# Down projection of 32 of 43 FFN tiles in seven-product blocks, with weight forms as sums

## The chip, the cores and the metric

The kernel runs on one core of one Trainium2 chip. The metric is the device time of one execution in microseconds, the median of several runs.

## What is computed

One step of a one-layer decoder trunk for 544 tokens (512 of a prompt and 8 x 4 of a decode batch), all in f32: a token-mixing sub-layer with one input and one output projection, cross-attention into memory tokens, and a gated feed-forward layer (FFN) with a causal convolution, each between two norms. The change concerns the last product of the FFN:

```python
def conv_ffn(x, prev, w_up, w_conv, w_down):
    h = x @ w_up
    ext = jnp.concatenate([prev.astype(h.dtype), h], axis=1)
    hc = causal_dwconv(ext, w_conv)
    g, u = jnp.split(hc, 2, axis=-1)
    return (jax.nn.silu(g) * u) @ w_down, ext[:, -(FFN_CONV_WIDTH - 1):]
```

D_MODEL is 2048 and D_FF is 5504, so w_down has 43 tiles of 128 rows and 16 tiles of 128 columns.

## The kernel before

Activations lie transposed, 128 features x 544 tokens in a tile. Every f32 operand of a matmul is split into a high and a low part in TensorE's own 32-bit format (L80 `split`: ScalarE (ACT) copies the high part, L82, VectorE (DVE) subtracts it for the low part, L83). A product takes three matmuls: high weight with high token, high with low, low with high (L156 `mm6`, its matmul is L162). The 544 tokens go through in two halves, so a weight tile costs six matmuls.

Weights stream from memory through SyncE's (SP's) DMA queue into four raw buffers of 256 KB, and are split ahead of their use (L91 `Weights`, L116 its load); `pair_tiles` (L88) gives four pairs of 128 x 1024 tiles for the parts.

The up projection of tiles 6 to 42 already works in units of seven products in place of eight (Strassen's scheme): L1102 loads 512 KB weight quarters, L1110 forms their sums on DVE, L1154 is its matmul with 272 tokens at a time, L1134 to L1168 take the products out of PSUM. The results, the gated tiles f of the FFN, go to a buffer in DRAM (fd) and come back when wanted (fr).

The down projection then runs over blocks of FFN tiles (8, 8, 8, 8, 7 and 4; `BLOCKS`). For each of 16 output chunks m, a PSUM tile `dn` of two banks collects a block: 8 tiles x 3 x 2 matmuls. In the first block ACT copies it into the SBUF accumulator `facc[m]` (L1244), in the next four DVE adds it there (L1246). `hidden` (L1209) loads and splits the next block's f tiles. The last block, of 4 tiles (`dl`), is followed by the final norm, the residual and the output. The order within each engine's queue is set when the program is built, by a scheduler; an engine takes its queue strictly in order, and PSUM tiles are ordered as whole tiles: work on one bank of a tile waits for an earlier read of its other bank. `background` and `spend` (L144) hand out work beside matmuls by a budget of estimated microseconds.

Of the kernel before, what the change touches and what calls it, by code (L numbers as in the profile page):

```python
# [22 lines left out]
KD = DM // P  # L23
# [4 lines left out]
NF = DFF // P  # L28
LAST = ((0, 288), (288, NT))
FB = 8  # L30
BLOCKS = (8, 8, 8, 8, 7, 4)
NMEM = 256
EPS = 1e-6
RAW, WHL = 4, 8
NH = NT // 2
# [9 lines left out]
def trunk_kernel(ctx: ExitStack, tc: tile.TileContext, I, O):  # L45
    nc = tc.nc
    dma = nc.sync.dma_start
# [3 lines left out]
    wp = ctx.enter_context(tc.tile_pool(name="wp", bufs=1))  # L51
# [28 lines left out]
    def split(hi, lo, src, scale=None):  # L80
        if scale is None:
            nc.scalar.activation(hi, src, AF.Copy)  # L82
            nc.vector.tensor_tensor(lo, src, hi.bitcast(F32), op=ALU.subtract)  # L83
        else:
            nc.scalar.activation(hi, src, AF.Copy, scale=scale)
            nc.vector.scalar_tensor_tensor(lo, src, scale, hi.bitcast(F32), op0=ALU.mult, op1=ALU.subtract)  # L86

    def pair_tiles(name):  # L88
        return tuple(wp.tile([P, 1024], F32R, tag=f"w{x}", bufs=WHL // 2, name=f"{name}{x}") for x in "hl")

    class Weights:  # L91
# [6 lines left out]
        def add(self, src, kind="split", n=512, fresh=False):  # L98
            self.specs.append((src, kind, n, fresh))
# [32 lines left out]
    W = Weights()  # L132
# [3 lines left out]
    background = []  # L136

    def pause(cost):

        return cost, lambda: None  # L140
# [146 lines left out]
    add_project(wup, warm_up[:-3], 3)  # L287
    add_project(wup, warm_up[-3:], 3)

    def add_down():  # L290
        for bi, blk in enumerate(blocks):
            if blk is blocks[-1]:
                for m in range(KD):
                    W.add(I["w_down"][9, m], "split" if m < WHL else "mov", fresh=m == 0)
            else:
                for ms in [range(3)] + [[m] for m in range(3, KD)]:
                    for kc in range(2):
                        for m in ms:
                            if len(blk) == FB or kc == 0:
                                W.add(I["w_down"][bi * 2 + kc, m])  # L300
                            else:
                                W.add(I["w_down_3"][m], n=3 * P)


    xs = [None] * KD
# [404 lines left out]
    q = [None] * NG  # L710
# [201 lines left out]
    facc = [None] * KD  # L912
    fd = [dram.tile([P, NT], F32, name=f"fd{i}") for i in range(NF)]
# [80 lines left out]
    todo = [(kc * 4 + kk, 1) for kc in range(4) for kk in range(4)]  # L994
    for si, (hf, kc) in enumerate(seq):
# [5 lines left out]
        for at, (kk, g) in enumerate(steps):  # L1001
            k = kc * 4 + kk
# [36 lines left out]
    def halves(t):  # L1039
        return t.rearrange("p (a t) -> p a t", a=2)  # L1040
# [146 lines left out]
    load(WARM)  # L1187
    todo = list(order)
    for at, (i, n) in enumerate(order):
        while len(order) - len(todo) < min(at + 4, len(order)):  # L1190
            make(*todo.pop(0))
        product(i, n)
        if i == NF - 1:
            if n == "S1":
                for j in range(8):
                    f_load(j)
            for j in {"S2": (0, 1), "A12": (2, 3), "S3": (4, 5), "A22": (6, 7)}.get(n, ()):
                f_split(j)
            if n == "A22":
                add_down()  # L1200
                W.fill(W.used + 5)
    fastp.close()


    down = ctx.enter_context(ExitStack())
    resp[0] = down.enter_context(tc.tile_pool(name="resp2", bufs=1, reuse_waits="tile"))
    aux16[0] = down.enter_context(tc.tile_pool(name="facc", bufs=1, reuse_waits="tile"))

    def hidden(bi):  # L1209
        fss[bi] = []  # L1210
        for i in blocks[bi]:
            f = tmp(f"fr{i}")[:, :NT]
            dma(f, fd[i])
            fss[bi].append(tuple((res if bi == len(blocks) - 1 else mov)(f"f{x}{i}", F32R) for x in "hl"))
            split(*fss[bi][-1], f)

    for bi, blk in enumerate(blocks):
        nb = len(blk)
        if bi + 1 < len(blocks):
            hidden(bi + 1)  # L1220
        fs = fss[bi]

        if bi < len(blocks) - 1:
            grp = list(range(3))
            pss = [mm_ps(f"dn{bi}_{m}") for m in grp]
            for kc in range(2):
                ws = [W.next() for m in grp]
                for kk in range(min(4, nb - kc * 4)):
                    k = kc * 4 + kk
                    for w, ps in zip(ws, pss):  # L1230
                        mm6(ps, w, fs[k], k == 0, k == nb - 1, kk)
            for m in range(KD):
                if m < 3:
                    ps = pss[m]
                else:
# [6 lines left out]
                if bi == 0:  # L1242
                    facc[m] = auxu(f"facc{m}")
                    nc.scalar.activation(facc[m], flat(ps), AF.Copy)  # L1244
                else:
                    nc.vector.tensor_tensor(facc[m], flat(ps), facc[m], op=ALU.add)  # L1246
        else:


# [1 line left out]
            wl = [W.next() for m in range(4)]  # L1251
# [46 lines left out]
            for half in LAST:  # L1298
                a, b = half
# [16 lines left out]
                for ms in pairs:  # L1316
                    ps = mm_ps(f"dl{ms[0]}_{a}")
# [125 lines left out]
```

## Time and profile before

| what | value |
|---|---|
| median of 3 runs | 2319.52 us (2318.92 to 2319.97) |
| the profiled execution's own time | 2319.19 us |
| its span in the trace | 2317.5 us |
| PE busy | 2270.2 us (98%) |
| DVE busy | 1535.1 us (66%) |
| ACT busy | 931.5 us (40%) |
| POOL busy | 418.0 us (18%) |
| mean DMA rate | 119 GB/s |

The profile is one execution; its time lies .33 us under the median. The span is what the trace covers, 1.7 us less than that execution's time. PE is TensorE's matmuls, PEld its weight loads, POOL is GpSimd, SP is SyncE. Shares are averages over all stages; a stage's own bound is read from a stretch of it.

### The profile page before, as it was taken

Reading aid. Unit: us, or ns where it says so; the run is one execution under the profiler, and the core shown is the slowest. Engines: PE = TensorE matmul, PEld = TensorE weight load, DVE = VectorE, ACT = ScalarE, POOL = GpSimd, SP = SyncE. Lnnn points to the kernel's source line nnn. Section 1 sums busy time; section 2 is a strip of 40 time slices with the busy share of each in tenths; the row PEclk is TensorE's granted clock in tenths of the full one; section 3 lists DMA queues with packets and bytes.
Section 4 is the critical chain, followed back from the end, with each engine's and each line's share of the span. In section 5 each row is a group of like instructions: output and inputs, shape, how many; then the busy total and the mean of one; then the engine's idle time right before and its main releaser. Section 6 shows DMA issues by size and latency. Waiting matters only on the chain.

```text
span 2317.5 us, 43666 instructions
## 1 busy us (share of the span) xinstructions
PE 2270.2 (98%) x17755; PEld 2245.8 (97%) x17755; DVE 1535.1 (66%) x2401; ACT 931.5 (40%) x1526; POOL 418.0 (18%) x516
## 2 busy tenths in 40 slices
PE   8999999999999999999999999999999999999995
PEld 8999999999989889999999999999999999999995
DVE  6775494543495888788888888888887233342347
ACT  6221222443354554445545555554545232131133
POOL 0000000000041453133233323333331000000005
PEclk9999999999999999999999999999999999999997
DMA  7323323333454555333333333333335333232242
GB/s 230 95 83 80 89 84 88 86 113 97 141 174 146 160 178 188 101 121 105 120 120 109 108 120 124 99 121 115 115 105 193 97 121 127 94 112 88 85 160 78
DMA packets 149065, 276.31 MB, mean 119 GB/s; under 512 B 30880, under 2 KB 42432, under 8 KB 148864
## 3 DMA queue, kind: packets, MB, share of 16 engines
q1 hardware_dynamic: 148864, 273.53, 38.0%
q8 instruction: 139, 2.28, 0.4%
q14 instruction: 62, 0.51, 0.1%
HBM read 249.81 MB, written 23.66 MB: 118 GB/s over the span
## 4 chain that ended last, share of the span: by engine, by line
PE 90%; DVE 5%; DMA 2%; issue 1%; ACT 1%; POOL 0%; SPq 0%; POOLq 0%; DVEq 0%; ACTq 0%
PE mm L162 31%; PE ab L1154 24%; PE dn L162 20%; PE c L1154 9%; PE dl L162 1%; PE xo L162 1%; PE kps L162 1%; PE sps L792 1%; DVE fxl L86 1%; DVE mix L823 1%; DVE mix L669 0%; DMA fr<-fd 0%; DVE xa L822 0%; PE sop L881 0%; DMA raw<-in_w_xq 0%
## 5 line engine op out<-in xcount | busy, mean ns | idle before, releaser
L1246 DVE TENSOR_TENSOR facc<-dn,facc 128x544 f32<-128x544 f32 x64 | 46.0, 723 | 213.8 <-PE dn L162 213.7
L941 POOL COPY fe<-fst 128x16 f32<-128x16 f32 x86 | 181.3, 2120 | 0.0
L951 POOL COPY fnp<-fe 128x2 f32<-128x2 f32 x86 | 42.4, 493 | 613.1 <-DVE fe L1138 531.6
L956 DVE SCALAR_TENSOR_TENSOR fa<-fe,fcw,fa 128x560 f32<-128x560 f32 x172 | 136.6, 795 | 0.5 <-ACT fa L954 0.3
L234 POOL TENSOR_TENSOR r_f<-r_f,mhalf 128x3 f32<-128x3 f32 (+1 forms) x2 | 1.6, 777 | 500.2 <-DVE r_f L233 500.2
L386 DVE SCALAR_TENSOR_TENSOR y<-eb,cv,y 128x512 f32<-128x512 f32 x120 | 88.6, 738 | 0.0
L954 ACT ACTIVATE fa<-fe,fcw 128x560 f32<-128x560 f32 x86 | 65.7, 764 | 38.2 <-DVE fe L1139 28.9
L261 POOL TENSOR_TENSOR ss<-ss,sq_h 128x544 f32<-128x544 f32 (+2 forms) x45 | 55.8, 1241 | 70.7 <-ACT sq_h L260 70.0
L950 POOL COPY fns<-fe 128x16 f32<-128x16 f32 x86 | 58.0, 674 | 6.6 <-DVE fe L985 0.8
L958 ACT ACTIVATE fa<-fa 128x560 f32<-128x560 f32 x43 | 28.9, 673 | 47.6 <-DVE fa L956 47.5
L1110 DVE TENSOR_TENSOR S<-A,A 128x1024 f32<-128x1024 f32 x37 | 45.4, 1226 | 1.2
L1110 DVE TENSOR_TENSOR A<-A,S 128x1024 f32<-128x1024 f32 x37 | 45.3, 1224 | 1.2
L1110 DVE TENSOR_TENSOR A<-A,A 128x1024 f32<-128x1024 f32 x37 | 45.1, 1218 | 0.0
L1110 DVE TENSOR_TENSOR S<-S,A 128x1024 f32<-128x1024 f32 x37 | 45.0, 1216 | 0.0
L234 POOL TENSOR_TENSOR r_gn<-r_gn,mhalf 128x5 f32<-128x5 f32 x4 | 4.7, 1170 | 179.4 <-DVE r_gn L233 179.4
L1138 DVE TENSOR_TENSOR fe<-c,u 128x240 f32<-128x240 f32 x74 | 29.7, 402 | 3.6 <-ACT u L1134 3.5
L261 POOL TENSOR_TENSOR ss<-ss,sq_xa 128x256 f32<-128x256 f32 (+1 forms) x26 | 23.0, 886 | 48.0 <-ACT sq_xa L260 47.9
L83 DVE TENSOR_TENSOR fl<-fr,fh 128x544 fp32r<-128x544 f32 x43 | 29.0, 720 | 3.3 <-ACT fh L82 3.3
L82 ACT ACTIVATE fh<-fr 128x544 fp32r<-128x544 f32 x43 | 27.3, 653 | 7.6 <-DMA fr<-fd 4.8
L1134 ACT ACTIVATE u<-ab 128x272 f32<-128x272 f32 x74 | 28.1, 380 | 4.9 <-PE ab L1154 4.9
L963 DVE TENSOR_TENSOR f<-fa,fa 128x512 f32<-128x512 f32 x43 | 29.4, 684 | 0.0
L388 DVE SCALAR_TENSOR_TENSOR y<-eb,cv,y 128x32 f32<-128x32 f32 x120 | 28.6, 239 | 0.0
(3958 smaller groups left out, 9333.5 us busy)
## 6 DMA issues: line engine op xcount, KB each, us to landing
A<-in_w_up SPq DMA_DIRECT2D x148, 512.0 KB, 3.5
raw<-in_w_down SPq DMA_DIRECT2D x160, 256.0 KB, 2.7
raw<-in_w_in SPq DMA_DIRECT2D x128, 256.0 KB, 2.7
raw<-in_w_out SPq DMA_DIRECT2D x64, 256.0 KB, 2.7
raw<-in_w_up SPq DMA_DIRECT2D x48, 256.0 KB, 2.9
fd<-f SPq DMA_DIRECT2D x43, 272.0 KB, 2.1
fr<-fd SPq DMA_DIRECT2D x43, 272.0 KB, 4.6
raw<-in_w_xo SPq DMA_DIRECT2D x32, 256.0 KB, 2.9
```

Of the source, the lines that this page charges most:

```text
L162: nc.tensor.matmul(ps[:, pa:pb], lhsT=a_, rhs=b_[:, a:b], start=start and q == 0, stop=stop and q == 2)
L261: (eng or nc.vector).tensor_tensor(dst, dst, sq[:, :n], op=ALU.add)
L386: nc.vector.scalar_tensor_tensor(acc[:, :NP], e[:, t:t + NP], w, acc[:, :NP], op0=ALU.mult, op1=ALU.add)
L941: nc.gpsimd.tensor_copy(smp6(e)[:, :, 0:2], st[:, j, gu])
L950: nc.gpsimd.tensor_copy(nst[:, j, gu], smp6(e)[:, :, 4:6])
L951: nc.gpsimd.tensor_copy(nsp[:, j, gu], e[:, NP:NP + 2])
L954: nc.scalar.activation(acc, e[:, 0:560], AF.Copy, scale=fcw[:, m, 0:1])
L956: nc.vector.scalar_tensor_tensor(acc, e[:, t:560 + t], fcw[:, m, t:t + 1], acc, op0=ALU.mult, op1=ALU.add)
L1110: nc.vector.tensor_tensor(out, a, b, op=op)
L1138: nc.vector.tensor_tensor(e[:, 2 + NH:2 + NP], bank[:, :NP - NH], add[:, :NP - NH], op=ALU.add)
L1154: nc.tensor.matmul(bank, lhsT=w[:, k * P:(k + 1) * P], rhs=t, start=start and k == 0 and q == 0, stop=k == 7 and q == 2, skip_group_check= ...
L1246: nc.vector.tensor_tensor(facc[m], flat(ps), facc[m], op=ALU.add)
```

## The change

`BLOCKS` becomes (7, 8, 8, 8, 8, 4). The first block, of 7 tiles, runs as before with ACT's copy into `facc`, the last block runs as before too. The four blocks of 8 tiles between them run as 16 units (block, q), q = 0 to 3, each for four output chunks. A unit takes its weights as four quarters A11, A12, A21, A22 of 128 x 1024 (512 KB), and the token halves of the tiles as four others, and makes seven products of 24 matmuls x 272 tokens in the order A12, D, G, A11, E, H, A21, in place of eight. The weight forms are sums:

- S is loaded as A21, and a DMA issued by POOL adds A22 into it in flight; D is S. E is A12 with A22 added in the same way (L1256 of the new text).
- G is S + A12, added on DVE (L1261).
- H is that sum + A11, added by a third accumulating DMA (L1265), issued behind G's split.

The products of a unit gather in two two-bank PSUM tiles (`da`: A12, G, E, A21; `db`: A11) and, for D and H, in two one-bank tiles `dc`; half p of `da` and `db` is one bank. ACT takes every half out with a sign (L1291, L1300), DVE adds the results into `facc` (L1294, L1301). The next block's token forms, seven high and low pairs for each of two tile pairs, are made beside units q = 2 and 3 (`fd_form`). The down weights lie in DRAM in a new order (`w_down_s`); a unit reads A12, A21 and A22 twice, and A11 twice.

```diff
-BLOCKS = (8, 8, 8, 8, 7, 4)
+BLOCKS = (7, 8, 8, 8, 8, 4)
...
+    def fd_form(bi, d, n):
+        x, y = halves(fr[bi][d]), halves(fr[bi][2 + d])
+        b11, b12, b21, b22 = x[:, :, :NH], x[:, :, NH:], y[:, :, :NH], y[:, :, NH:]
+        if n == 1:
+            nc.vector.scalar_tensor_tensor(b22, b22, -1.0, b21, op0=ALU.mult, op1=ALU.subtract)
+        if n == 2:
+            nc.vector.tensor_tensor(b22, b11, b22, op=ALU.add)
+        if n == 4:
+            nc.vector.tensor_tensor(b21, b21, b11, op=ALU.subtract)
+        if n == 6:
+            nc.vector.scalar_tensor_tensor(b22, b22, -1.0, b12, op0=ALU.mult, op1=ALU.subtract)
+        src = (b22, b22, b22, b12, b21, b11, b22)[n]
+        TD[bi, n, d] = h, l = mov(f"d{n}h{d}", F32R), mov(f"d{n}l{d}", F32R)
+        nc.scalar.activation(halves(h), src, AF.Copy)
+        nc.vector.tensor_tensor(halves(l), src, halves(h).bitcast(F32), op=ALU.subtract)
...
+    dsteps = ("A12", "D", "G", "A11", "E", "H", "A21")
...
+    def d_load(u):
+        for n, *parts in (("A12", "A12"), ("S", "A21", "A22"), ("A11", "A11"), ("E", "A12", "A22"), ("A21", "A21")):
+            t = draws[u, n] = rawd.tile([P, 1024], F32, tag="rawd", bufs=8, name=f"{n}_{u[0]}_{u[1]}")
+            dma(t, d_src(u, parts[0]))
+            for a in parts[1:]:
+                nc.gpsimd.dma_start(t, d_src(u, a), accum_op=ALU.add)
+
+    def d_make(u, n):
+        s = draws[u, "S"]
+        if n == "G":
+            nc.vector.tensor_tensor(s, s, draws[u, "A12"], op=ALU.add)
+        dmade[u, n] = pair_tiles(f"{n}_{u[0]}_{u[1]}")
+        split(*dmade[u, n], s if n in ("D", "G", "H") else draws[u, n])
+        if n == "G":
+            nc.gpsimd.dma_start(s, d_src(u, "A11"), accum_op=ALU.add)
+
+    def d_product(u, n):
...
+        which = {"A11": "b", "D": "c", "H": "c"}.get(n, "a")
+        for p in range(2):
+            m = 4 * q + 2 * p
+            t = dbank[u, which]
+            bank = t[p][:, :NH] if which == "c" else t[:, p * 512:p * 512 + NH]
+            for k in range(4):
+                th, tl = (t_[:, k % 2 * NH:(k % 2 + 1) * NH] for t_ in TD[bi, dsteps.index(n), k // 2])
+                for i, (w, t) in enumerate(((wh, th), (wh, tl), (wl, th))):
+                    nc.tensor.matmul(bank, lhsT=w[:, (4 * p + k) * P:(4 * p + k + 1) * P], rhs=t,
...
+            for at, (u, n) in enumerate(dorder):
+                while len(dorder) - len(todo) < min(at + 4, len(dorder)):
+                    i = units.index(todo[0][0])
+                    while loaded <= min(i + (todo[0][1] == "E"), len(units) - 1):
+                        d_load(units[loaded])
+                        loaded += 1
+                    d_make(*todo.pop(0))
+                d_product(u, n)
+                if u[0] + 1 < len(blocks) - 1:
+                    if u[1] == 1 and n == "A12":
+                        fd_in(u[0] + 1)
+                    if u[1] == 2 and n == "G":
+                        for _, f in fd_work(u[0] + 1, [0]):
+                            f()
+                    if u[1] == 3 and n != "A21":
+                        for _, f in fd_work(u[0] + 1, [dsteps.index(n) + 1]):
+                            f()
```

The changed program's queues at three places, in unit (1, 2), an ordinary one; in names, da1_2 is tile `da` of block 1, q = 2, and what stands in brackets is what a row waits for.

PE before, at the seam of two output chunks (dn2_5 is chunk 5 of the third block):

```order
L162 MATMUL dn2_5_22960<-fl23_21649,w394h_22751 128x256
L162 MATMUL dn2_5_22960<-fl23_21649,w394h_22751 128x288
L162 MATMUL dn2_5_22960<-fh23_21648,w394l_22752 128x256
L162 MATMUL dn2_5_22960<-fh23_21648,w394l_22752 128x288
L162 MATMUL dn2_6_23020<-fh16_21606,w396h_22761 128x256 [waits DVE_49,Activation_49]
L162 MATMUL dn2_6_23020<-fh16_21606,w396h_22761 128x288
L162 MATMUL dn2_6_23020<-fl16_21607,w396h_22761 128x256
```

PE now, the end of G's first half, four matmuls of A11, and G's second half:

```order
L1284 MATMUL da1_2_22020<-d2h1_21270,G_1_2l_21984 128x272
L1284 MATMUL db1_2_22141<-d3h0_21366,A11_1_2h_22016 128x272
L1284 MATMUL db1_2_22141<-d3l0_21367,A11_1_2h_22016 128x272
L1284 MATMUL db1_2_22141<-d3h0_21366,A11_1_2l_22017 128x272 [waits DVE_49]
L1284 MATMUL db1_2_22141<-d3h0_21366,A11_1_2h_22016 128x272
L1284 MATMUL da1_2_22020<-d2h0_21157,G_1_2h_21983 128x272 [waits Activation_49]
L1284 MATMUL da1_2_22020<-d2l0_21158,G_1_2h_21983 128x272
```

A chunk of before starts in a tile of its own. Now the second half of G waits for ACT, which reads the first half's bank of the same tile, and four matmuls of the next product, A11, have been put between.

ACT before, in the third block (w396h is the high part of a weight pair):

```order
L82 ACTIVATE w396h_22761<-raw396_22759 128x512 [waits DMAHW2_49,DVE_49,PE_49]
L82 ACTIVATE w396h_22761<-raw397_22841 128x512 [waits DMAHW3_49]
L82 ACTIVATE w398h_22871<-raw398_22869 128x512 [waits DMAHW4_49,DVE_49,PE_49]
L82 ACTIVATE w398h_22871<-raw399_22901 128x512 [waits DMAHW5_49]
L82 ACTIVATE w400h_22931<-raw400_22929 128x512 [waits DMAHW6_49,DVE_49,PE_49]
```

ACT now, around the high split of H (kc_1_10 reads D's second half, ka0_1_8 the first half of G, ka0_1_10 of A12 and G the second):

```order
L82 ACTIVATE E_1_2h_22061<-E_1_2_21812 128x1024 [waits DMASW7_49,PE_49,Activation_49]
L1291 ACTIVATE ka0_1_10_22047<-da1_2_22020 128x272 [waits PE_49]
L1300 ACTIVATE kc_1_8_22079<-dc1_2_0_22065 128x272 [waits PE_49]
L82 ACTIVATE H_1_2h_22097<-S_1_2_21807 128x1024 [waits DMASW1_49,PE_49,Activation_49]
L1300 ACTIVATE kc_1_10_22094<-dc1_2_1_22066 128x272 [waits PE_49]
L1291 ACTIVATE ka0_1_8_22033<-da1_2_22020 128x272 [waits PE_49]
L82 ACTIVATE A21_1_2h_22137<-A21_1_2_21815 128x1024 [waits DMAHW4_49,DVE_49,PE_49]
L1291 ACTIVATE ka0_1_10_22047<-da1_2_22020 128x272 [waits PE_49]
```

Before, ACT only split weights in these blocks. Now it also takes out all products, and H's split, which waits for the accumulating DMA, stands ahead of kc_1_10 and ka0_1_8.

DVE now, from the sum for G on:

```order
L1261 TENSOR_TENSOR S_1_2_21807<-S_1_2_21807,A12_1_2_21805 128x1024 [waits DVE_49]
L1294 TENSOR_TENSOR facc2_20570<-facc2_20570,ka1_1_4_21934 128x544 [waits Activation_49]
L83 TENSOR_TENSOR G_1_2l_21984<-S_1_2_21807,G_1_2h_21983 128x1024 [waits PE_49,Activation_49]
L83 TENSOR_TENSOR A11_1_2l_22017<-A11_1_2_21810,A11_1_2h_22016 128x1024 [waits DMAHW2_49,PE_49,Activation_49]
L1294 TENSOR_TENSOR facc3_20571<-facc3_20571,ka1_1_6_21948 128x544 [waits Activation_49]
L83 TENSOR_TENSOR E_1_2l_22062<-E_1_2_21812,E_1_2h_22061 128x1024 [waits DMASW7_49,PE_49,Activation_49]
L1301 TENSOR_TENSOR facc4_20572<-facc4_20572,kc_1_8_22079 128x272 [waits Activation_49]
L83 TENSOR_TENSOR H_1_2l_22098<-S_1_2_21807,H_1_2h_22097 128x1024 [waits DMASW1_49,PE_49,Activation_49]
```

The sum, G's low split behind it, then splits of A11 and E and adds into `facc`; before, DVE had only low splits and the adds of L1246 here.

POOL now (in these blocks before, its queue holds nothing):

```order
L1256 DMA S_1_2_21807<-in_w_down_s 128x1024 [waits DMAHW1_49,DMASW4_49,DVE_49]
L1265 DMA S_1_1_21551<-in_w_down_s 128x1024 [waits DVE_49]
L1256 DMA E_1_2_21812<-in_w_down_s 128x1024 [waits DMAHW4_49,DMAHW3_49]
L1256 DMA S_1_3_22051<-in_w_down_s 128x1024 [waits DMASW6_49,DMAHW6_49,DMASW0_49,DVE_49]
L1265 DMA S_1_2_21807<-in_w_down_s 128x1024 [waits DMASW1_49,DVE_49]
L1256 DMA E_1_3_22056<-in_w_down_s 128x1024 [waits DMAHW0_49,DMASW2_49]
L1256 DMA S_2_0_22313<-in_w_down_s 128x1024 [waits DMASW3_49,DMAHW3_49,DMASW1_49,DVE_49]
```

The third transfer of a unit (L1265) stands behind the first one of the next unit and waits for DVE.

## Rows read from the trace of the kernel before

**Rows 1.** The page: busy time by engine, and the granted clock by slice.

```profile
PE 2270.2 (98%) x17755; PEld 2245.8 (97%) x17755; DVE 1535.1 (66%) x2401; ACT 931.5 (40%) x1526; POOL 418.0 (18%) x516
...
PEclk9999999999999999999999999999999999999997
```

**Rows 2.** The page: the chain that ended last, by engine and line.

```profile
PE 90%; DVE 5%; DMA 2%; issue 1%; ACT 1%; POOL 0%; SPq 0%; POOLq 0%; DVEq 0%; ACTq 0%
PE mm L162 31%; PE ab L1154 24%; PE dn L162 20%; PE c L1154 9%; PE dl L162 1%; PE xo L162 1%; PE kps L162 1%; PE sps L792 1%; DVE fxl L86 1%; DVE mix L823 1%; DVE mix L669 0%; DMA fr<-fd 0%; DVE xa L822 0%; PE sop L881 0%; DMA raw<-in_w_xq 0%
```

**Rows 3.** The chain in order of time: start us, us, what.

```profile
1730.39 12.26 PE ab L1154 x96
...
1748.67 3.01 PE c L1154 x24
...
1788.28 452.01 PE dn L162 x3600
2240.29 28.35 PE dl L162 x216
```

**Rows 4.** Table of stretches: PE, PEld, DVE, ACT, POOL busy us, PEclk, DMA share, GB/s.

```profile
1100.00:1121.29 21.29, 21.29 (x170) 21.14 (x169) 17.61 (x23) 10.79 (x15) 6.47 (x8) 1.00 0.35 114
...
1869.00:2240.30 371.30, 371.30 (x2962) 371.30 (x2961) 132.64 (x211) 83.75 (x147) 0.00 (x0) 1.00 0.32 102
```

**Rows 5.** Timelines of PE, then ACT, at the last up unit: start us, us, work.

```profile
1762.77 0.29 PE L1154 MATMUL ab<-t5h,S_42l 128*128 128x272 f32 x1
1763.55 0.40 PE L1154 MATMUL ab<-t6h,A_42h 128*128 128x272 f32 x1 [0.49 <-ACT u L1134]
1763.78 0.29 PE L1154 MATMUL ab<-t6l,A_42h 128*128 128x272 f32 x1
...
1763.10 0.40 ACT L1134 ACTIVATE u<-ab 128x272 f32<-128x272 f32 x1 [4.03 <-PE ab L1154]
```

**Rows 6.** Timelines of DVE and ACT, then a group of the page.

```profile
1738.77 0.43 DVE L1162 TENSOR_TENSOR fe<-ab,t 128x272 f32<-128x272 f32 x1
...
1743.77 1.22 DVE L83 TENSOR_TENSOR S_42l<-S,S_42h 128x1024 fp32r<-128x1024 f32 x1
...
1754.59 1.06 ACT L82 ACTIVATE S_42h<-A 128x1024 fp32r<-128x1024 f32 x1 [0.30 <-PE ab L1154]
1755.55 0.38 ACT L1134 ACTIVATE u<-ab 128x272 f32<-128x272 f32 x1
1755.83 0.65 ACT L82 ACTIVATE fh<-fr 128x544 fp32r<-128x544 f32 x1
...
L1246 DVE TENSOR_TENSOR facc<-dn,facc 128x544 f32<-128x544 f32 x64 | 46.0, 723 | 213.8 <-PE dn L162 213.7
```

**Rows 7.** The page's DMA queues and issues, then landing times of the 512 KB loads.

```profile
q1 hardware_dynamic: 148864, 273.53, 38.0%
q8 instruction: 139, 2.28, 0.4%
...
A<-in_w_up SPq DMA_DIRECT2D x148, 512.0 KB, 3.5
raw<-in_w_down SPq DMA_DIRECT2D x160, 256.0 KB, 2.7
...
DMA to landing us min/median/max: 3.3/3.5/6.2
```

**Rows 8.** POOL's copies by line: ns min/median/max.

```profile
L941 POOL COPY fe<-fst x86: 193/1872/5752, 862.5 to 1754.8; 128x16 f32<-128x16 f32 x86
```

**Rows 9.** Timelines of SP, DVE and PE at the start of the down stage.

```profile
1776.98 4.21 SPq L1213 DMA_DIRECT2D fr<-fd  x7
...
1764.04 1.29 DVE L83 TENSOR_TENSOR w320l<-raw,w320h 128x512 fp32r<-128x512 f32 x2
1767.82 0.69 DVE L83 TENSOR_TENSOR w322l<-raw,w322h 128x512 fp32r<-128x512 f32 x1 [2.48 <-ACT w322h L82]
...
1769.68 0.41 PE L162 MATMUL dn<-fh,w320h 128*128 128x256 f32 x2
```

More of the change, by code (lines that the diff above doesn't have):

```diff
@@ L288, in trunk_kernel, with add_down_first, add_down_last @@
     add_project(wup, warm_up[-3:], 3)
[L290 to L302, printed above, removed]
+    def add_down_first():
+        for ms in [range(3)] + [[m] for m in range(3, KD)]:
+            for kc in range(2):
+                for m in ms:
+                    if kc == 0:
+                        W.add(I["w_down"][0, m])
+                    else:
+                        W.add(I["w_down_3"][m], n=3 * P)
+    def add_down_last():
+        for m in range(KD):
+            W.add(I["w_down"][1, m], "split" if m < WHL else "mov", fresh=m == 0)
     xs = [None] * KD
@@ L1194, in trunk_kernel @@
             if n == "S1":
-                for j in range(8):
+                for j in range(len(blocks[0])):
                     f_load(j)
-            for j in {"S2": (0, 1), "A12": (2, 3), "S3": (4, 5), "A22": (6, 7)}.get(n, ()):
+            for j in {"S2": (0, 1), "A12": (2, 3), "S3": (4, 5), "A22": (6,)}.get(n, ()):
                 f_split(j)
             if n == "A22":
-                add_down()
+                add_down_first()
                 W.fill(W.used + 5)
@@ new lines, in trunk_kernel, with fd_in @@
+    TD, fr = {}, {}
+    def fd_in(bi):
+        fr[bi] = []
+        for o in (0, 4):
+            for d in range(2):
+                t = frp.tile([P, 2 * NT], F32, tag="fr", bufs=4, name=f"fr{bi}_{o}_{d}")
+                for j in range(2):
+                    dma(t[:, j * NT:(j + 1) * NT], fd[blocks[bi][2 * d + o + j]])
+                fr[bi].append(t)
+    def fd_form(bi, d, n):
[13 more added lines that the diff above has]
+        nc.vector.tensor_tensor(halves(l), src, halves(h).bitcast(F32), op=ALU.subtract)
@@ new lines, in d_make, with keep, add @@
+    def d_make(u, n):
[7 more added lines that the diff above has]
+    def d_product(u, n):
+        bi, q = u
+        if n == "A12":
+            dbank[u, "a"] = mm_ps(f"da{bi}_{q}")
+        if n == "A11":
+            dbank[u, "b"] = mm_ps(f"db{bi}_{q}")
+        if n == "D":
+            dbank[u, "c"] = [aux_ps(f"dc{bi}_{q}_{p}") for p in range(2)]
+        wh, wl = dmade.pop((u, n))
+        which = {"A11": "b", "D": "c", "H": "c"}.get(n, "a")
[7 more added lines that the diff above has]
+                    nc.tensor.matmul(bank, lhsT=w[:, (4 * p + k) * P:(4 * p + k + 1) * P], rhs=t,
+                                     start=n in ("A12", "A11", "D") and k == 0 and i == 0, stop=k == 3 and i == 2,
+                                     skip_group_check=True)
+            def keep(kind, half, sign):
+                if (u, p, kind) not in dkeep:
+                    dkeep[u, p, kind] = tmp(f"k{kind}_{bi}_{m}")[:, :NT]
+                nc.scalar.activation(dkeep[u, p, kind][:, half * NH:(half + 1) * NH], bank, AF.Copy, scale=sign)
+            def add(m_, kind):
+                nc.vector.tensor_tensor(facc[m_], facc[m_], dkeep.pop((u, p, kind)), op=ALU.add)
+            if n == "A12":
+                keep("a0", 1, 1.0)
+            elif n == "D":
+                t = wp.tile([P, 512], F32, tag="raw", bufs=RAW, name=f"kc_{bi}_{m}")[:, :NH]
+                nc.scalar.activation(t, bank, AF.Copy, scale=-1.0)
+                nc.vector.tensor_tensor(facc[m + 1][:, :NH], facc[m + 1][:, :NH], t, op=ALU.add)
+            elif n == "G":
+                keep("a0", 0, -1.0)
+                add(m, "a0")
+            elif n == "A11":
+                keep("bc", 1, 1.0)
+            elif n == "E":
+                keep("a1", 0, 1.0)
+            elif n == "H":
+                keep("bc", 0, 1.0)
+                add(m, "bc")
+            else:
+                keep("a1", 1, -1.0)
+                add(m + 1, "a1")
@@ L1213, in hidden, with fd_work @@
             dma(f, fd[i])
-            fss[bi].append(tuple((res if bi == len(blocks) - 1 else mov)(f"f{x}{i}", F32R) for x in "hl"))
+            fss[bi].append(tuple(res(f"f{x}{i}", F32R) for x in "hl"))
             split(*fss[bi][-1], f)
+    def fd_work(bi, ns):
+        return [(2.2 if n in (1, 2, 4, 6) else 1.5, lambda n=n, d=d: fd_form(bi, d, n)) for n in ns for d in range(2)]
+    facc2 = [faccp.tile([P, 2 * NT], F32, name=f"facc{p}") for p in range(KD // 2)]
+    facc = [facc2[m // 2][:, m % 2 * NT:(m % 2 + 1) * NT] for m in range(KD)]
+    fd_in(1)
+    background.extend([pause(4.0)] + fd_work(1, range(4)))
     for bi, blk in enumerate(blocks):
         nb = len(blk)
-        if bi + 1 < len(blocks):
-            hidden(bi + 1)
+        if bi == len(blocks) - 1:
+            hidden(bi)
+        if bi not in (0, len(blocks) - 1):
+            continue
         fs = fss[bi]
-        if bi < len(blocks) - 1:
+        if bi == 0:
             grp = list(range(3))
@@ L1241, in trunk_kernel @@
                             mm6(ps, w, fs[k], k == 0, k == nb - 1, kk)
[L1242 to L1246, printed above, removed]
+                nc.scalar.activation(facc[m], flat(ps), AF.Copy)
+                spend(1.2)
+            spend(1e9)
+            for _, f in fd_work(1, range(4, 7)):
+                f()
+            units = [(b_, q) for b_ in range(1, len(blocks) - 1) for q in range(4)]
+            todo = [(u, n) for u in units for n in dsteps]
+            dorder = list(todo)
+            loaded = 0
+            for at, (u, n) in enumerate(dorder):
[14 more added lines that the diff above has]
+                        for _, f in fd_work(u[0] + 1, [dsteps.index(n) + 1]):
+                            f()
+                elif u[1] == 3 and n == "A11":
+                    add_down_last()
+                    W.ahead = 0
+                    W.fill(W.used + 4)
+            downp.close()
+            resp[0] = down.enter_context(tc.tile_pool(name="resp2", bufs=1, reuse_waits="tile"))
+            aux16[0] = down.enter_context(tc.tile_pool(name="aux17", bufs=1, reuse_waits="tile"))
         else:
@@ L1377 @@
     wd = x["w_down"][0]
-    wd4 = np.concatenate([wd[:36 * P], wd[39 * P:]])
+    wd4 = np.concatenate([wd[:4 * P], wd[39 * P:]])
     ins = {
```

16 lines of the change are left out of this document (12 added, 4 removed).

## The prediction

> **What bounds the kernel now.** Read the page's first two parts before anything else: TensorE (PE) is busy in 98% of the span and its granted clock stands at 9 or more tenths in every slice but the last [rows 1]. The chain that ended last says which PE work carries the end: 90% of it is PE, and 20% are the matmuls of the down projection, L162 into dn [rows 2]. In order of time the chain holds one unbroken piece of 452.01 us with 3600 of the 3744 dn matmuls, up to 2240.29 [rows 3]. That is 452.01 / 3600 = 0.1256 us per matmul with nothing between. The table of stretches shows why nothing else can take time off there: between 1869 and 2240.3, PE is busy for 371.30 of 371.30 us at granted clock 1.00, beside it DVE for 132.64, ACT for 83.75, POOL not at all, and the DMA engines for a share of 0.32 [rows 4]. So this stage pays for matmuls alone, and helpers have two thirds of their time free. The change takes matmuls out and gives the free engines work; the question is which wait the new work brings into PE's queue.
>
> The sum is made against the profiled execution, 2319.19 us; the median of the runs shown is 2319.52, 0.33 above. A measurement of this kernel can tell 0.2% from no change, 4.6 us.
>
> **Matmuls removed.** Blocks 1 to 5 of before become one direct block of 7 tiles, 7 x 16 x 3 x 2 = 672 matmuls, and 16 units of 7 products x 2 x 4 x 3 = 168. Direct blocks of 39 tiles take 39 x 96 = 3744; now there are 672 + 2688 = 3360. 384 fewer x 0.1256 = **-48.2 us**. Of 272 columns, 24 matmuls take 3.01 us in the chain, 0.1254 each [rows 3], so a unit of 168 back to back is 21.07 us.
>
> **What a unit of this form loses.** The nearest rows are the up projection's units, which have the same 168 matmuls and 7 products: one goes from 1730.39 to 1748.67 + 3.01 = 1751.68, 21.29 us [rows 3], and so .22 us above the back-to-back time. That is the lower bound, 16 x .22 = 4 us. In the new order five second halves per unit (A12, G, A11, E, A21) stand behind ACT's read of the other half of the same two-bank tile; D and H have a tile for each half and do not wait. What such a wait costs without cover is seen at the end of the up stage, where cover runs out: the last matmul into half b starts at 1762.77, ACT's read starts at 1763.10 and takes .40, the next matmul starts at 1763.55 and takes .40 instead of .29 [rows 5]. The distance is .78 where .13 is normal: .65 lost, and .1 more because the next start, 1763.78, is .23 later instead of .13. The new order puts four or five matmuls of the next product, .50 to .62 us, into the gap; so .65 - .50 = .15 remains with four and little with five, and the restart of .1 is paid each time. Five times .15 to .25, and now and then a 1.06 us split ahead of the read on ACT [rows 6], give 1.1 us per unit: **+17.6 us** for 16. Upper bound without any cover: 5 x .75 = 3.75 per unit, +60.
>
> **DVE and ACT.** The evacuation by DVE (64 x .723, [rows 6]) goes. A unit has on DVE seven low splits and S+A12, 8 x 1.22, six adds of 544 x .72, two of 272 x .43: 15.0 us of some 22. On ACT seven high splits x 1.06 and fourteen reads x .38: 12.7 us. Both fit, so this costs nothing as long as products are made ahead; three products of lead are 9 us. The last unit of a block adds the token forms of the next one, twenty DVE instructions of 544 x .72 = 14.4 us: 29.4 of 22, so DVE falls 7 us behind, inside the lead. I charge 0 for the three such units; the upper bound is 3 x 7.4 = 22.
>
> **The ends.** At the start of the stage five token loads now stand ahead of the first weight load on SP; seven of them took 4.21 us, so five take 3.0 [rows 9]. The first weight's low split had ended at 1764.04 + 1.29 = 1765.33 and was used at 1769.68, 4.35 us later, which covers them; the next weight's low split started only at 1767.82, so the bounds are 0 and 3, and I take .5. At the end a split of the last block's tokens, one high (about .65) and one low (.72), stands in PE's way before the last half of A21: 1.4 us with nothing behind to hide it. In sum **+2 us**.
>
> **The accumulating transfers.** Of three per unit, two (L1256) have most of a unit of slack, as the loads are issued a unit ahead. L1265, S += A11, has not: it can be issued only when G's low split has read S, and H's high split waits for it. On ACT that split stands in front of kc_1_10 and ka0_1_8, the read of G's first half, and PE's second half of G waits for the latter. So a late transfer stops PE by the queue of ACT, long before H itself is wanted. By hand, from a unit's first matmul: E's last matmul is the 139th, 139 x .1254 + four waits of .25 = 18.4; then D high 1.06, D low 1.22, two adds 1.44, S+A12 1.22, G high 1.06, G low 1.22, in sum 7.2. G low ends at 25.6, that is 3.5 us into the next unit of 22.1. The transfer lands L later. Then H high 1.06, two reads of .38 and hand-over, 1.9 together: second half of G possible at 5.4 + L. PE wants it after 76 matmuls and two waits, at 76 x .1254 + .5 = 10.0. **Up to L = 4.6 us it is free; each us above costs 16 us in all.**
>
> No transfer in before accumulates or is issued by POOL; all data go through hardware queues [rows 7]. So L is bounded: below by a plain 512 KB load, 3.3 at best and 3.5 in the median; above by its slowest, 6.2, or by two plain ones in a row, 7.0 [rows 7]. I take the row nearest in kind: 256 KB take 2.7 and 512 KB take 3.5, so each 256 KB more adds .8; a sum that reads its target too moves twice the bytes, 3.5 + 2 x .8 = 5.1, as an estimate. (5.1 - 4.6) x 16 = **+8 us**. The ends give 0 and (7.0 - 4.6) x 16 = +38.
>
> The Trainium skill, page "DMA: Bandwidth & Descriptors", section "Anatomy of one DMA — SWDGE (gpsimd) path", fits a POOL-issued transfer as 2.0 us plus bytes at 436 GB/s, an estimate of 3.2 us for 512 KB. By that figure L would be free and the sum -29; no run so far shows such a transfer.
>
> **Sum:** -48.2 + 17.6 + 0 + 2 + 8 = -20.6 us, about **2298.5 us**.
>
> **Rivals.** (a) *The sum in flight is as cheap as a load*, L below 4.6: -48.2 + 17.6 + 2 = -28.6, 2290.5 us. For it: 3.5 us for plain loads at a DMA share of 0.32 [rows 4, 7]. Against: two reads per write. Chance .22. If besides this the covers work as in the up units, -48.2 + 4 + 2 = -42, 2277 us, of which I give .04.
>
> (b) *The transfer's start is held up.* POOL must start it while DVE has A11's low split, an add and E's low split in its queue behind G's, 1.22 + .72 + 1.22 = 3.2 us. If POOL can't work beside DVE, L is 5.1 + 3.2 = 8.3, the head of ACT's queue waits, and the time is -28.6 + 16 x 3.7 = +30.6, 2350 us. It becomes slower than before from L = 4.6 + 28.6 / 16 = 6.4 on. For it: beside a busy DVE, POOL's copy of 128x16 has a minimum of 193 ns, a median of 1872 and a maximum of 5752 [rows 8]. Against: those copies move data themselves, starting a transfer does not, and DVE is busy here for two thirds of the time, against 17.6 of 21.3 there [rows 4]. Chance .20 for a result above before by this or by a slow sum (L of 6.7 and more), half of it below 2335.
>
> The Trainium skill, page "SBUF — State Buffer", section "SBUF: two separate sides", has a rule that speaks for (b): DVE and GpSimd share a port pair as an exclusive lock, and a POOL-issued DMA can starve for descriptors; it tells of 620 ns becoming 3100. The stretched copies agree with a lock, but no row of before shows a descriptor waiting.
>
> (c) *No difference*: L of 6.1 to 6.7, within 4.6 us of 2319. Chance .10. That the change doesn't take its matmuls out isn't a case: the new order holds 384 rows fewer.
>
> (d) *DVE's extra in the last units isn't absorbed*, +22 us on the sum: about 2320 us. Against: nine us of lead. Chance .04, shared by same and slower.
>
> **How the numbers follow.** Forecast (L of 4.6 to 6.1, 2291 to 2314): .40. With (a) .22 and its extreme .04, faster is .66; (c) and half of (d) give .12 for the same; (b) and the rest of (d) .22 for slower. The range goes from 2287, leaving out the extreme of (a), to 2335, the half of (b) with L up to 7.4 (+16): some .8 of the chances. The likeliest case's own range is 2291 to 2314.
>
> **What would show it.** PE rows fall by 384. A regular unit, first matmul to first matmul, should take 22.1 to 23 us. PE's waits should be five short ones on ACT per unit, and the one on ka0 before G's second half the longest. From issue to landing, L1265 should take about 5 us; 3.5 or less means (a). H's high split should start within .1 us of the landing, with kc and ka0 right behind it. If POOL's issue comes microseconds after G's low split ends, (b) is right; if H's split is never late and PE still loses more than 2 us per unit, the cover term is wrong. A granted clock below 1.00 in these stretches, or units longer in blocks' last quarter alone, would make the reasoning wrong in another place.

## The result and the profile after

The changed kernel is slower: 2343.11 us in the median of 4 runs (2339.9 to 2346.5) against 2319.74 us for the kernel before in the same comparison (4 runs). The ratio is 1.010, with an interval from 1.0083 to 1.0118. The profiled execution took 2346.5 us, its span is 2344.3 us, 26.8 us more than the span of before.

The page after, its busy times, clock, DMA queues and issues:

```profile
PE 2258.1 (96%) x17371; PEld 2216.8 (95%) x17371; DVE 1673.2 (71%) x2521; ACT 1057.6 (45%) x1758; POOL 444.4 (19%) x564
...
PEclk9999999999999999999999999999999999999998
...
q0 software_dynamic: 6912, 25.17, 6.3%
...
A<-in_w_down_s SPq DMA_DIRECT2D x48, 512.0 KB, 6.6
...
S<-in_w_down_s POOLq DMA_DIRECT2D x32, 512.0 KB, 6.7
```

Against [rows 1], PE has 384 matmuls fewer, as wanted, and is busy for 12.1 us less; but its share of the span went from 98% to 96%. PE is no longer always busy, so the time is in its waits. The POOL-issued transfers have a queue of their own, q0, and land 6.7 us after their issue in the median. The slices of the clock line are too coarse here: the table of stretches shows it (PE, PEld, DVE, ACT, POOL busy us, PEclk, DMA share, GB/s). Its rows are the 16 units together (up to the first matmul of the last block, which starts 9 matmuls before the units' last one), one unit of the 16, the stretch behind that unit's long wait, and another unit:

```profile
1855.73:2264.69 408.96, 370.75 (x2679) 354.65 (x2677) 265.59 (x323) 212.91 (x382) 37.94 (x43) 0.95 0.67 172
1905.43:1933.33 27.90, 24.66 (x171) 23.80 (x169) 14.15 (x18) 11.87 (x21) 2.64 (x3) 0.88 0.61 152
1918.90:1924.50 5.60, 5.60 (x25) 5.60 (x26) 3.23 (x5) 1.74 (x3) 0.89 (x1) 0.50 0.43 155
2012.09:2036.53 24.44, 22.33 (x170) 21.32 (x169) 14.13 (x18) 11.76 (x21) 2.66 (x3) 1.00 0.71 173
```

The first row is to be compared with the last of [rows 4]: there PE was busy all the time at clock 1.00, here for 370.75 of 408.96 us at 0.95. The third has clock 0.50, the lower of the two levels: 25 matmuls in 5.60 us.

The chain of waits of this execution breaks off 7 us before the end and says nothing of this stage, so the list of PE's waits takes its place, here between 1855 and 2245 (us in total, times, longest):

```profile
PE da L1284 <- ACT ka L1291: 28.9, 12, 3.5
PE dc L1284 <- ACT H_0h L82: 5.3, 2, 2.7
PE dc L1284 <- DVE H_0l L83: 2.2, 3, 0.7
```

And one such wait, in unit (1, 2), engine by engine. These are timelines: DVE's low splits of G and A11, POOL's third transfer (L1265) and the accumulating one for E behind it, SP's next load (the next unit's A21), ACT around H's high split, and PE before G's second half:

```profile
1907.79 1.23 DVE L83 TENSOR_TENSOR G_2l<-S,G_2h 128x1024 fp32r<-128x1024 f32 x1 [0.55 <-ACT G_2h L82]
1908.94 1.22 DVE L83 TENSOR_TENSOR A_2l<-A,A_2h 128x1024 fp32r<-128x1024 f32 x1
...
1909.43 0.88 POOL L1265 DMA_DIRECT2D S<-in_w_down_s  x1 [7.62 <-DVE G_2l L83]
1910.69 0.88 POOL L1256 DMA_DIRECT2D E<-in_w_down_s  x1 [0.39 <-issue]
...
1910.18 0.33 SPq L1254 DMA_DIRECT2D A<-in_w_down_s  x1
...
1917.20 1.06 ACT L82 ACTIVATE H_2h<-S 128x1024 fp32r<-128x1024 f32 x1 [4.33 <-DMA S<-in_w_down_s]
1918.16 0.38 ACT L1300 ACTIVATE kc<-dc 128x272 f32<-128x272 f32 x1
1918.44 0.39 ACT L1291 ACTIVATE ka<-da 128x272 f32<-128x272 f32 x1
...
1915.37 0.28 PE L1284 MATMUL db<-d3h,A_2h 128*128 128x272 f32 x1
1918.88 0.60 PE L1284 MATMUL da<-d2h,G_2h 128*128 128x272 f32 x1 [3.23 <-ACT ka L1291]
1919.28 0.43 PE L1284 MATMUL da<-d2l,G_2h 128*128 128x272 f32 x1
1919.50 0.43 PE L1284 MATMUL da<-d2h,G_2l 128*128 128x272 f32 x1
```

The waits list names ACT's read `ka` as the culprit, but the timeline shows that this read took .39 us and was itself behind the split of H, which stood idle for 4.33 us for the transfer. The transfer was issued at 1909.43 and H began at 1917.20. SP's load waits in the program for A11's low split, the next one on DVE, and starts as that ends, at 1910.18. Behind the wait PE's matmuls start .22 us apart, where .125 is normal.

The distances from one matmul's start to the next, added up over the 16 units, give the whole account. What goes beyond .1254 us per matmul is sorted into long waits (a distance over .6 us), stretches at clock 0.50, and short waits and restarts (the rest). In the changed kernel it is 40.7, 14.3 and 18.4 us, in sum 73.4. With 384 matmuls fewer at -48.2 and about 2 us at the two ends this is +27, against 26.8 in the spans. (The profiled execution is the longest of the four; the medians lie 23.4 us apart. Where a slow stretch is taken to begin and end moves up to 1.2 us between the half clock and the short waits, here and in the table below.)

### The profile page after: what moved, and what is told of

Read it like the earlier page. It is cut to its first block, busy times and chain, and to the rows that moved or that the text cites. A ratio compares the mean times of both kernels' runs of the same rounds, so it can differ in the third digit from the quotient of the medians.

```text
span 2344.3 us, 43259 instructions
## 1 busy us (share of the span) xinstructions
PE 2258.1 (96%) x17371; PEld 2216.8 (95%) x17371; DVE 1673.2 (71%) x2521; ACT 1057.6 (45%) x1758; POOL 444.4 (19%) x564
## 5 line engine op out<-in xcount | busy, mean ns | idle before, releaser
L940 POOL COPY fe<-fst 128x16 f32<-128x16 f32 x86 | 168.1, 1966 | 0.0
L1291 ACT ACTIVATE ka<-da 128x272 f32<-128x272 f32 x128 | 48.5, 388 | 22.2 <-PE da L1284 21.8
L957 ACT ACTIVATE fa<-fa 128x560 f32<-128x560 f32 x43 | 28.9, 673 | 48.3 <-DVE fa L955 48.2
L1294 DVE TENSOR_TENSOR facc<-facc,ka 128x544 f32<-128x544 f32 x64 | 46.1, 720 | 5.8 <-ACT ka L1291 5.8
L1256 POOL DMA_DIRECT2D S<-in_w_down_s x16 | 14.3, 892 | 183.3 <-DMA S<-in_w_down_s 51.2
L1265 POOL DMA_DIRECT2D S<-in_w_down_s x16 | 14.5, 906 | 180.3 <-DVE G_3l L83 58.2
L85 ACT ACTIVATE fxh<-mix,gains 128x256 fp32r<-128x256 f32 (+1 forms) x32 | 16.5, 517 | 29.4 <-DVE mix L822 29.4
```

The source lines that it names most:

```text
L940: nc.gpsimd.tensor_copy(smp6(e)[:, :, 0:2], st[:, j, gu])
L1291: nc.scalar.activation(dkeep[u, p, kind][:, half * NH:(half + 1) * NH], bank, AF.Copy, scale=sign)
L1294: nc.vector.tensor_tensor(facc[m_], facc[m_], dkeep.pop((u, p, kind)), op=ALU.add)
```

## The experiments

Theory 1, which is the prediction's own mechanism with another size: the third transfer lands later than I took it to, H's split holds up ACT's queue and that holds up PE, and behind the pauses PE runs at half clock. Theory 2: ACT and DVE are too full or H's data are late wherever the split stands. For the lateness itself there are two more: 1a, adding in flight is what costs; 1b, the neighbours in flight do. Each account below is worked out from the run's own trace as above (us beyond .1254 per matmul in the 16 units):

| kernel | median us | ratio to before (interval) | long waits | short waits, restarts | half clock |
|---|---|---|---|---|---|
| the change | 2343.11 | 1.010 (1.0083 to 1.0118) | 40.7 | 18.4 | 14.3 |
| e1, H's sum on DVE | 2292.26 | 0.988 (0.9867 to 0.9900) | 1.8 | 19.3 | 0.0 |
| e2, ACT's reads first | 2312.96 | 0.997 (0.9964 to 0.9984) | 17.0 | 17.5 | 6.8 |
| e3, plain transfer | 2298.72 (one run) | | 5.1 | 20.5 | 1.4 |
| e4, without A21's load | 2315.21 (one run) | | 22.7 | 18.9 | 1.5 |
| e5, sum on DVE and banks | 2279.08 | 0.983 (0.9809 to 0.9842) | 2.6 | 3.6 | 0.0 |
| e6, banks alone | 2295.83 | 0.990 (0.9877 to 0.9916) | 15.0 | 3.2 | 6.2 |

**Without the transfer.** The sum is made by DVE, from A11's tile that is loaded anyway.

```diff
-        if n == "G":
-            nc.gpsimd.dma_start(s, d_src(u, "A11"), accum_op=ALU.add)
+        if n == "A11":
+            nc.vector.tensor_tensor(s, s, draws[u, "A11"], op=ALU.add)
```

> The third sum of a unit, S += A11, is made by a DVE add behind A11's split in place of the accumulating transfer. Theory 1 (the transfer's lateness stops PE through the head of ACT's queue, and the pauses then halve PE's clock): the 16 long waits (40.7 us in the changed kernel's trace) and the slow stretches (14.4 us) go, the short waits of about 1.1 us per unit stay; units of 22.2 us, granted clock 1.00 in the down stage, about 2290 us. Theory 2 (ACT and DVE are too full, the transfer only happens to be the last to arrive): DVE gets 1.22 us more per unit, the long waits stay or move to H's low split, units of 25 us or more, 2335 to 2350 us.

Measured: 2292.26 us, and theory 1 holds: units of 22.2 to 22.4 us in the ordinary case, no long wait in them (two of .9 us are left, in the first unit and at the end of the last), and the clock at 1.00 over all 16:

```profile
1854.64:2211.58 356.94, 355.10 (x2678) 339.45 (x2676) 282.44 (x340) 212.78 (x382) 24.64 (x28) 1.00 0.61 173
1897.99:1920.40 22.41, 22.40 (x171) 21.36 (x170) 15.29 (x19) 11.84 (x21) 1.78 (x2) 1.00 0.60 165
```

DVE does 17 us more in these units than in the changed kernel (282.44 against 265.59) and the kernel is 51 us faster. So DVE's load was not the bound, and one add of 1.22 us replaces a transfer of 7. From the end of G's low split to H's high one 4.6 us pass now, in unit (1, 2) from 1901.56 to 1906.18:

```profile
1900.34 1.22 DVE L83 TENSOR_TENSOR G_2l<-S,G_2h 128x1024 fp32r<-128x1024 f32 x1 [0.55 <-ACT G_2h L82]
...
1903.26 1.22 DVE L1265 TENSOR_TENSOR S<-S,A 128x1024 f32<-128x1024 f32 x1
...
1906.18 1.06 ACT L82 ACTIVATE H_2h<-S 128x1024 fp32r<-128x1024 f32 x1 [0.77 <-ACT kc L1300]
```

**With the transfer, but nothing behind it.** H's split is kept behind ACT's reads by a dependence, and products are made three ahead.

```diff
-                while len(dorder) - len(todo) < min(at + 4, len(dorder)):
+                while len(dorder) - len(todo) < min(at + 3, len(dorder)):
...
+        if n == "H":
+            g0 = gread[u]
+            nc.vector.tensor_tensor(dmade[u, n][0][:, :2], g0, g0, op=ALU.subtract)
...
             elif n == "G":
+                if p == 0:
+                    gread[u] = dkeep[u, p, "a0"][:, :2]
```

> The accumulating transfer stays, but H's high split stands behind ACT's reads of D's second and G's first half (a two-column DVE write into H's tile, which depends on G's read, keeps it there; products are made three ahead in place of four). Theory 1: the transfer lands as late as before (about 7 us after its issue), but PE no longer waits before G's second half; what is left is a wait at H's first matmuls of 0 to 1 us per unit, the clock stays at 1.00, about 2295 to 2310 us. Theory 2 (PE waits for the data of H itself, wherever it stands): the waits only move from G to H and keep their size, 2.5 us per unit, 2335 to 2350 us.

Measured: 2312.96 us, a few us past theory 1's upper end and far from theory 2's. The transfer is as late as in the changed kernel (the transfer's own rows: ns of an issue and us from issue to landing, min/median/max), and yet an ordinary unit runs at full speed (the stretches below, first unit (1, 2)). What remains sits in the first unit of each block (second, unit (2, 0)):

```profile
L1268 POOL DMA_DIRECT2D S<-in_w_down_s x16: 872/882/1244, 1853.7 to 2214.5; - x16
...
DMA to landing us min/median/max: 5.1/6.9/9.5
```

```profile
1904.20:1926.72 22.52, 22.41 (x170) 21.35 (x169) 14.30 (x18) 11.65 (x21) 2.63 (x3) 1.00 0.75 190
1947.41:1977.36 29.95, 25.14 (x182) 24.29 (x181) 22.53 (x31) 15.88 (x30) 2.63 (x3) 0.94 0.85 228
```

In the ordinary unit H's split waits too, but only itself. The timeline of ACT there shows the reads of D (kc) and G (ka) done before it:

```profile
1912.35 0.40 ACT L1303 ACTIVATE kc<-dc 128x272 f32<-128x272 f32 x1 [0.69 <-PE dc L1287]
1913.85 0.40 ACT L1294 ACTIVATE ka<-da 128x272 f32<-128x272 f32 x1 [1.11 <-PE da L1287]
1915.55 1.06 ACT L82 ACTIVATE H_2h<-S 128x1024 fp32r<-128x1024 f32 x1 [1.30 <-DMA S<-in_w_down_s]
```

So the place in ACT's queue is what turned a late transfer into a late PE. (Making products three ahead was not tried by itself; it doesn't bring the transfer forward, since G's low split ends 3.5 to 3.9 us into an ordinary unit, as late as in the changed kernel.) In the first units of blocks 2 to 4 G's low split ends 8.0 us into the unit, because DVE still has the token forms to finish, and the transfer lands 9.4 and 8.2 us after its issue beside token loads in blocks 2 and 3 and 7.5 us after it in block 4, which has none: there H itself is late. With block 1's first unit, where it takes 9.5 us, they hold 16.5 of the 17.0 us of long waits and all 6.8 us at half clock.

**A plain transfer in the same place.** H is A11 alone there.

```diff
-            nc.gpsimd.dma_start(s, d_src(u, "A11"), accum_op=ALU.add)
+            nc.gpsimd.dma_start(s, d_src(u, "A11"))
```

> The third transfer of a unit overwrites S with A11 in place of adding to it; everything else stays. (H is then A11 alone, and the output is not the reference's.) Theory 1a (the lateness is the price of adding in flight: the target is read too): issue to landing falls from about 7.0 to 4 to 4.5 us, H's split is in time and the long waits go, 2290 to 2300 us. Theory 1b (the lateness comes from the loads in flight beside it and from the queue, not from adding): landing stays at 6 to 7 us, and the time within 8 us of the changed kernel's.

Measured, the third transfer's issue time and landing:

```profile
L1265 POOL DMA_DIRECT2D S<-in_w_down_s x16: 553/564/919, 1851.7 to 2197.7; - x16
...
DMA to landing us min/median/max: 3.5/3.7/7.2
```

This is as theory 1a had it: 3.7 us in the median, even lower than its 4 to 4.5, and a time of 2298.72 us. A plain transfer that POOL issues takes .2 us more than SP's 3.5 [rows 7]; adding in flight is what costs. POOL's issue is also shorter, .56 us against .88.

**Without the neighbour.** The load of A21 is left out and its product takes A11's tile.

```diff
-        for n, *parts in (("A12", "A12"), ("S", "A21", "A22"), ("A11", "A11"), ("E", "A12", "A22"), ("A21", "A21")):
+        for n, *parts in (("A12", "A12"), ("S", "A21", "A22"), ("A11", "A11"), ("E", "A12", "A22")):
...
-        split(*dmade[u, n], s if n in ("D", "G", "H") else draws[u, n])
+        split(*dmade[u, n], s if n in ("D", "G", "H") else draws[u, "A11" if n == "A21" else n])
```

> The load of A21 into its own tile is left out, and the product A21 takes A11's tile (the output is not the reference's). In the changed kernel this load starts .8 us after the third transfer in 11 of 16 units, and these transfers take 6.5 to 8 us; where it starts 1.4 us after or not at all they take 5.3. Theory 1b (neighbours in flight): the third transfer lands 5.3 us after its issue in most units, the long waits fall to about 1 us, the clock stays at 1.00, about 2300 us. Theory 1a (adding costs 7 us by itself): landing stays near 7 us and the time within 8 us of the changed kernel's.

Measured:

```profile
L1265 POOL DMA_DIRECT2D S<-in_w_down_s x16: 872/872/898, 1851.1 to 2212.7; - x16
...
DMA to landing us min/median/max: 5.1/5.3/8.8
```

Both 1a and 1b are true, each for a part. Without the load an added transfer takes 5.3 us where a plain one takes 3.7 even beside it: 1.6 us for adding. The changed kernel's 7.0 holds 1.7 us more. The run by itself doesn't say that these are the load's, since it moves another neighbour too: E's accumulating transfer, which POOL issues 1.2 to 1.8 us behind the third one in most units of the changed kernel, is issued 4 us or more ahead of it here. The last run below settles it: there E's transfer comes 1.0 to 1.3 us behind in ten units and the third lands in 5.1 to 5.4 us all the same. The landing came out as theory 1b said; the time, 2315, did not (about 2300): with the start of the transfer .41 us behind G's low split, 5.7 us pass until H may begin in the median, 1.1 more than the 4.6 that were free, and the units other than the first ones of blocks 2 and 3 lose 1.1 us each on average to long waits; those two wait 2.8 and 4.4 us beside token loads. But the half clock is down to 1.5 us.

**Other PSUM banks.** Both banks of a unit's first halves lie in one tile, those of the second halves in another.

```diff
-            dbank[u, "a"] = mm_ps(f"da{bi}_{q}")
-        if n == "A11":
-            dbank[u, "b"] = mm_ps(f"db{bi}_{q}")
+            dbank[u, "ab"] = [mm_ps(f"da{bi}_{q}_{p}") for p in range(2)]
...
-            t = dbank[u, which]
-            bank = t[p][:, :NH] if which == "c" else t[:, p * 512:p * 512 + NH]
+            t = dbank[u, "c" if which == "c" else "ab"][p]
+            bank = t[:, 512:512 + NH] if which == "b" else t[:, :NH]
```

With H's sum on DVE as well:

> As the run with H's sum on DVE, and the PSUM banks of a unit are dealt out anew: both banks of first halves (of products a and b) lie in one two-bank tile, those of second halves in the other, so that ACT's read of a first half no longer stands before the second half of the same product. Theory 1 (the 1.1 to 1.3 us of short waits and restarts per unit come from that order alone): units of 168 matmuls take 21.1 to 21.3 us, about 18 us less in all, 2273 to 2277 us. Theory 2 (they come from ACT being behind with its reads): ACT has the same 12.7 us of work in a shorter unit, short waits of about the same sum appear before other products, 2286 to 2293 us.

Measured: 2279.08 us, 40 us below the kernel before and the fastest here. A unit is down to 21.33 us, and the short waits from 19.3 to 3.6 us in 16 units, as theory 1 has it:

```profile
1897.55:1918.88 21.33, 21.33 (x170) 21.19 (x169) 15.27 (x18) 12.20 (x21) 1.78 (x2) 1.00 0.61 175
```

The gain over e1 is 13 us, not 18: the expectation took all the short waits away, where 3.6 us of them stay; long ones are .8 us more (1.3 us in the first units of blocks 2 and 3), and about 1 us is lost behind the units. Alone:

> Only the PSUM banks are dealt out anew, the accumulating transfer stays. The short waits go as in the run with both. Theory 1 (the landing of the third transfer sets the pace of a unit): PE reaches the blocked place a microsecond earlier and waits longer there; G's low split ends about as long after the unit before, so units stay near 25 us and the time within 10 us of the changed kernel's 2343, 2333 to 2345 us. Theory 2 (the two losses simply add): about 18 us less than the changed kernel, 2325 us.

Measured: 2295.83 us, 47 us below the changed kernel, and both numbers are missed. The two losses neither add up nor replace each other; 12 units have no long wait at all, though the transfer is still there (unit (1, 2), an ordinary one, and (2, 0), then the transfer's landing):

```profile
1899.82:1921.06 21.24, 21.24 (x171) 21.21 (x170) 14.23 (x17) 12.20 (x21) 2.64 (x3) 1.00 0.78 197
1942.39:1970.06 27.67, 23.38 (x170) 23.14 (x169) 20.84 (x26) 14.58 (x25) 2.63 (x3) 0.88 0.81 223
```

```profile
DMA to landing us min/median/max: 5.1/5.3/8.7
```

Two things moved. First, the start: no matmuls of the next product stand between the halves any more, so E ends earlier. In the timelines of PE, the last matmul of E of unit (1, 1) starts at 1901.68 in the changed kernel, 3.75 us before the next unit; here at 1893.68, 6.14 us before it:

```profile
1893.68 0.28 PE L1282 MATMUL da<-d4h,E_1l 128*128 128x272 f32 x1
```

With E its weight tiles come free, D's split can go, and G's low split ends .56 us into the unit in place of 3.58. That is 3.0 us more for the transfer. Second, the landing: on DVE an add into `facc` now stands between G's low split and A11's, so SP's load of A21, which waits for the latter, starts 1.4 to 1.6 us after the transfer's issue, not .8, and the landing is 5.3 us, not 7.0. DVE and SP in unit (1, 2), where the transfer is issued at 1900.79:

```profile
1899.15 1.23 DVE L83 TENSOR_TENSOR G_2l<-S,G_2h 128x1024 fp32r<-128x1024 f32 x1 [0.55 <-ACT G_2h L82]
1900.29 0.72 DVE L1292 TENSOR_TENSOR facc<-facc,ka 128x544 f32<-128x544 f32 x1
1901.03 1.23 DVE L83 TENSOR_TENSOR A_2l<-A,A_2h 128x1024 fp32r<-128x1024 f32 x1
...
1902.29 3.33 SPq L1254 DMA_DIRECT2D A<-in_w_down_s  x2
```

The matmuls which hid a short wait had held back the end of the product that everything else waited for.

## Why the prediction was wrong

It said 2298.5 us with a range from 2287 to 2335, and 2343.11 came out: the wrong sign, and past the range. By its steps:

- **Matmuls removed, -48.2 us**: right. 384 rows are gone and a matmul of 272 columns costs .1254 us at full clock.
- **What a unit loses, +17.6 us**: right, 18.4 measured in the changed kernel and 19.3 in e1. In unit (1, 2) of e1 there are five such places, with .26 to .30 us from one start to the next and .23 to the one after, close to the .15 and .1 that the prediction put on top of .13. That these are reads of the other bank is shown by e5 and e6, where 3.6 and 3.2 remain.
- **DVE and ACT, 0**: right as an amount of work (e1 does more on DVE and is faster), but the lag behind a block's last unit is not free while a transfer hangs on it: G's low split ends at 6.06 us in place of 3.58 in the first units of blocks 2 to 4 of the changed kernel, and two of the three have the longest waits, 3.7 us each in sum.
- **The ends, +2 us**: about 2 measured.
- **The accumulating transfers, +8 us**: here the prediction failed. The working by hand was right up to the price: G's low split was to end 3.5 us into the next unit and ends at 3.58; 4.6 us were to be free, and in e1, where H begins 4.6 us after that split, no long wait is left. But L was put at 5.1 us, and between G's low split and H's high one lie 5.8 to 8.4 us in the units after the first, eight of the 15 between 7.0 and 7.6. "3.5 + 2 x .8 = 5.1" priced a transfer alone, and for that it was good: 5.3. It left out the .41 us from the split to the start of the issue, and the neighbour: SP's load of A21, which the next split on DVE sets free, costs 1.7 us more. Even the bound of 7.0 us, two plain loads in a row, was passed in six units. The long waits took 40.7 us, not 8.
- **The clock, which had no term at all**: the prediction took 1.00 throughout and named a lower one only as a sign of error. Behind nine of the long waits PE ran at 0.50 for some 3.4 to 6.8 us; this took 14.3 us. No ordinary unit without a long wait shows it, in any of the runs, though the same transfers and splits go on there; single waits of 1.9 us and less never brought it. By subtraction it is the difference between a result that the range held (about 2329) and the one that came.

The Trainium skill, page "DMA: Bandwidth & Descriptors", section "Anatomy of one DMA — SWDGE (gpsimd) path", has a fit that makes an estimate of 3.2 us for a POOL-issued 512 KB. e3's plain transfer agrees roughly, with 3.7 us; for one that adds it is too low by 2 us even without the load beside it.

Rival (b) came nearest in size, +30.6 at an L of 8.3, but its cause is refuted; the slow sum, which shared its chance of .20 and had no working of its own, is what came. POOL's issue starts .41 us behind G's low split in 14 of 16 units, and takes .88 us, between 875 and 1244 ns, beside a busy DVE:

```profile
L1265 POOL DMA_DIRECT2D S<-in_w_down_s x16: 875/884/1244, 1853.3 to 2244.9; - x16
...
DMA to landing us min/median/max: 5.3/7.0/9.4
```

The Trainium skill, page "SBUF — State Buffer", section "SBUF: two separate sides", tells of GpSimd unable to write descriptors while DVE runs an operation in a two-port mode. These rows show no such hold-up beside DVE's two-input f32 splits and adds. Rival (a)'s time, 2290.5 us, is what e1 reached (2292.26): without the late transfer the other terms of the sum hold to 2 us.

## What to carry to other kernels

Price a transfer from the place it will stand in: what is issued within the same microsecond, and what is behind its waiter on the waiter's engine; then give the pause it makes on PE a second price, for the clock afterwards. If an add of 1.22 us on an engine with time to spare can take the place of an accumulating transfer on a short chain, it should. Matmuls put into a gap aren't free: they push back the end of the product they interrupt, and whatever takes its tiles next.

## What was not expected of the hardware

- An accumulating 512 KB transfer costs POOL .88 us to issue, a plain one .56, and lands 5.3 us after its issue in place of 3.7.
- Beside another load it lands later, and .7 us of that load's start decide. Where SP's load of A21 is issued .8 us after it, in ten units of the changed kernel, it takes 6.5 to 7.7 us; where the load comes 1.4 to 1.6 us after, 5.1 to 5.4 us in units of the changed kernel and of e6 without token loads. The 4 KB packets in the traces show how. The transfer's own packets (queue q0) start 1.6 us behind its issue. In the ten units the load's (q1) begin 2.7 to 3.6 us behind it, and the two queues' packets run side by side; in the other units they begin 4.4 to 4.9 us behind it, as the transfer's last ones run. Here are packets, MB and share of 16 engines: 3 us of unit (1, 2) in the changed kernel, from 1912.40, then 2.9 us of it in e6, from 1902.40:

```profile
q0 software_dynamic: 94, 0.37, 64.8%
q1 hardware_dynamic: 81, 0.33, 31.2%
...
q0 software_dynamic: 126, 0.50, 100.1%
q1 hardware_dynamic: 1, 0.00, 0.4%
```

- A packet that adds takes .33 us, a plain one of the same transfer .16 (medians of the third transfer in the changed kernel and in e3). In e3 the transfer's last packets start about 3.1 us behind its issue, before the load's have well begun, and a load .8 us after it changes little (3.6 to 3.8 us in nine of ten units). Why .7 us of the load's start decide between side by side and one after the other was not tried.
- Behind a long wait of 2.1 us or more the granted clock fell to 0.50 in nine of 13 units of the changed kernel, and matmuls started .227 us apart; it was not tried what PE would have to do in the pause to keep it.
